# Low parts of the MLP weights: an adding transfer onto the negated rounded part instead of a VectorE difference

## The chip, the core and the metric

The kernel runs on one core of a Trainium2 chip. The metric is the device time of one execution in microseconds (us); the lower the better. TensorE (PE), VectorE (DVE), ScalarE (ACT), GpSimd (POOL) and SyncE (SP, which here only issues transfers) run side by side and wait for each other by semaphores; 16 DMA engines move the data.

## The reference

A model of three blocks over 512 tokens of width 1024 in float32. Two blocks hold a mixer (mLSTM and a convolution branch) and an MLP, each under a modulation that comes from a conditioning vector; a third block has a windowed attention and a gated convolution. What the change touches is the MLP of the two first blocks:

```python
for l in range(DEPTH):                      # DEPTH = 2
    mod = c_act @ w_ada[l] + b_ada[l]       # six vectors of 1024
    ...                                     # mixer
    h = rms_norm(x, g_pre_mlp[l]) * (1 + sc_mlp) + sh_mlp
    f = jnp.square(jax.nn.relu(h @ w_ff1[l])) @ w_ff2[l]   # 1024 -> 4096 -> 1024
    x = x + gt_mlp * rms_norm(f, g_post_mlp[l])
```

## The kernel before

**Split products.** Every large product of float32 numbers is made from three fast ones. A number is split into a rounded part h (type float32r) and a low part lo = x - h, and `mm3` (L163) accumulates h*h, h*lo and lo*h in PSUM. Activations are split where they are made, weights where they are loaded.

**A weight unit.** `wunit` (L145) makes one unit of 128 x 1024 numbers, 512 KB: SP loads it into `raw`, one of three buffers of the ring `wr`; ACT rounds it into `h` (ring `wh`, four buffers, L155); `sub` (L142) writes `lo = raw - h` (ring `wl`, four buffers, L143) on DVE, or on POOL where `eng=P` is given. The raw buffer is free when the difference is done. A unit then feeds 24 matmuls of 512 columns. After the unit `wunit` calls `step()`.

**Gemvs beside the products.** `step()` advances a list `pending` of generators, which compute the modulation of later stages. Most are gemvs (L348): each step loads 512 KB of `w_ada` or `w_mod_2` into the same ring `wr` (L352), and DVE scales it and adds it to an accumulator (L360, L362), once for `w_ada` and twice for the two vectors of `mod2_pairs`. A gate's gemv ends in a row that POOL broadcasts to all partitions (L413). In the first MLP `pending` holds gemvs of 8, 16, 16 and 8 steps. In the second it holds gemvs of 8 and 16 steps and then 24 steps of `expand_bias`, small copies between DRAM tensors that use no raw buffer.

**The MLP** (`mlp`, L534). `proj_first` uses four units that the mixer's end has loaded. `ff1(c)` computes eight tiles of the hidden layer with `projA` (L247): for each group of 256 columns two units, one for each half of the 1024 inputs, then 16 x 3 matmuls into two PSUM banks; `cons` applies Relu and Square on ACT and splits the result on DVE. `projB_chunk` (L289) multiplies finished hidden tiles with `w_ff2`: one unit feeds four PSUM banks, one for each 128 tokens. The order is ff1 chunks 0 and 1, a `projB_chunk` of 8 tiles, ff1 chunk 2, 8 tiles, ff1 chunk 3, 10 tiles. Then come `reload()` of x, `drain()` of what is pending and `projB_tail` (L310), whose six units lie in buffers outside the rings; during it the units of the next stage are loaded.

**Order.** SP issues in program order (a manual schedule). On the other engines the framework's scheduler sets the order, and the buffer that each tile gets from a ring, by its own estimates when the kernel is built; each engine then executes its queue in order.

Of the kernel before, what the change touches and what calls it, by code (L numbers as in the profile page):

```python
# [8 lines left out]
F32 = mybir.dt.float32  # L9
F32R = mybir.dt.float32r  # L10
BF16 = mybir.dt.bfloat16
I32 = mybir.dt.int32
AF = mybir.ActivationFunctionType
ALU = mybir.AluOpType
# [32 lines left out]
def fused_blocks_kernel(ctx: ExitStack, tc: tile.TileContext, I, out):  # L47
    nc = tc.nc
    V, S, P, PE, SP = nc.vector, nc.scalar, nc.gpsimd, nc.tensor, nc.sync
    act = S.activation  # L50
# [17 lines left out]
    def A(shape, dt=F32, name="a"):  # L68
        if not free_slots:
            raise RuntimeError(str(sorted(t.name for _, t in slot_of.values())))  # L70
        s = free_slots.pop(0)
        t = ap.tile(shape, dt, tag=f"A{s}", name=name)
        slot_of[id(t)] = (s, t)
        return t

    def HL(n, name):
        return A([128, 2, n], F32R, name)

    def free(*ts):
        for t in ts:  # L80
            free_slots.append(slot_of.pop(id(t))[0])
# [4 lines left out]
    def t2(shape, dt=F32, name="t2"):  # L86
        return t2p.tile(shape, dt, tag="t2", name=name)
# [4 lines left out]
    def mm():  # L92
        return mmp.tile([128, 512], F32, tag="mm", name="mm")
# [36 lines left out]
    def step():  # L130
        while pending:
            try:
                next(pending[0])
                return
            except StopIteration:
                pending.pop(0)

    def drain():
        while pending:
            step()  # L140

    def sub(dst, x_, h, eng=None):  # L142
        (eng or V).tensor_tensor(dst, x_, h.bitcast(F32), op=ALU.subtract)  # L143

    def wunit(src, a, b, eng=None, slots=False):  # L145

        raw = wrp.tile([128, a, b], F32, tag="wr", name="wr")
        SP.dma_start(raw, src)
        if slots:
            h = A([128, a, b], F32R, "wha")  # L150
            lo = A([128, a, b], F32R, "wla")
        else:
            h = whp.tile([128, a, b], F32R, tag="wh", name="wh")
            lo = wlp.tile([128, a, b], F32R, tag="wl", name="wl")
        S.copy(h, raw)  # L155
        sub(lo, raw, h, eng)
        step()
        return h, lo

    def unitsA(wv, c0, eng=None):  # L160
        return [wunit(wv[:, u * 4:u * 4 + 4, c0:c0 + 256], 4, 256, eng) for u in range(wv.shape[1] // 4)]

    def mm3(ps, ah, al, bh, bl, first, last):  # L163
        PE.matmul(ps, ah, bh, start=first, stop=False)  # L164
        PE.matmul(ps, ah, bl, start=False, stop=False)  # L165
        PE.matmul(ps, al, bh, start=False, stop=last)  # L166
# [69 lines left out]
    def mmA(ps, units, m, hT, view=lambda v: v, us=None):  # L236

        n = len(units)
        c = slice(m * 128, m * 128 + 128)
        for u in us or range(n):  # L240
            h, lo = units[u]
            for kk in range(4):
                kt = 4 * u + kk
                mm3(view(ps), h[:, kk, c], lo[:, kk, c], view(hT[kt][:, 0]), view(hT[kt][:, 1]),
                    kt == 0, kt == 4 * n - 1)

    def projA(wv, cols, hT, consumer, eng=None):  # L247

        ps = []
        for c0 in cols:  # L250
            un = unitsA(wv, c0, eng)
            pp = [mm(), mm()]
            for m in range(2):
                mmA(pp[m], un, m, hT)
            ps += pp
        consumer(ps)
# [17 lines left out]
    def proj_first(units, hT, between, consumer, perm=False):  # L274

        ps = [mm() for _ in range(2 * len(units))]
        for hf in range(2):
            def view(v, hf=hf):
                return grid(v)[:, :, 4 * hf:4 * hf + 4] if perm else v[:, hf * 256:hf * 256 + 256]

            for u in range(2):
                for ci, un in enumerate(units):
                    for m in range(2):
                        mmA(ps[2 * ci + m], un, m, hT, view, (u,))
            if hf == 0:
                between()
        consumer(ps)

    def projB_chunk(wv, kts, acts, evac, eng=None, hook=None):  # L289

        nk = len(kts)
        for n in range(2):
            ps = [mm() for _ in range(4)]
            for u in range(nk // 2):
                k0 = kts[2 * u]
                h, lo = wunit(wv[:, k0:k0 + 2, n * 512:n * 512 + 512], 2, 512, eng)
                for t in range(4):
                    for k in range(2):
                        kk = 2 * u + k
                        a = acts[kts[kk]]  # L300
                        mm3(ps[t], a[:, 0, t * 128:t * 128 + 128], a[:, 1, t * 128:t * 128 + 128],
                            h[:, k], lo[:, k], kk == 0, kk == nk - 1)
                if hook:
                    hook()
            if n == 1:
                free(*(acts[k] for k in kts))
            for t in range(4):
                evac(t, n, ps[t])

    def projB_tail(wv, kts, acts, y, G, eng=None, scale=1.0, prefetch=None, post=None):  # L310

        nk = len(kts)
        units = [[wunit(wv[:, kts[2 * u]:kts[2 * u] + 2, n * 512:n * 512 + 512], 2, 512, eng, True)
                  for u in range(nk // 2)] for n in range(2)]
        if prefetch:
            prefetch()
        for t in range(4):
            ps = [mm(), mm()]
            if t == 3 and post:
                post(-1)  # L320
            for n in range(2):
                for kk in range(nk):
                    h, lo = units[n][kk // 2]
                    a = acts[kts[kk]]
                    mm3(ps[n], a[:, 0, t * 128:t * 128 + 128], a[:, 1, t * 128:t * 128 + 128],
                        h[:, kk % 2], lo[:, kk % 2], kk == 0, kk == nk - 1)
            if t == 3:
                for un in units:
                    for h, lo in un:
                        free(h, lo)  # L330
                free(*(acts[kts[kk]] for kk in range(nk)))
            for n in range(2):
                c = slice(n * 512, n * 512 + 512)
                V.tensor_tensor(y[t][:, c], ps[n], y[t][:, c], op=ALU.add)
            yg = [t2([128, 512], F32, "yg") for _ in range(2)]
            for n in range(2):
                c = slice(n * 512, n * 512 + 512)
                V.tensor_tensor(yg[n], y[t][:, c], G[:, c], op=ALU.mult)
            r = row_rstd(y[t], scale)
            for n in range(2):  # L340
                c = slice(n * 512, n * 512 + 512)
                V.scalar_tensor_tensor(x[t][:, c], yg[n], r, x[t][:, c], op0=ALU.mult, op1=ALU.add)
            free(y[t])
            if post:
                post(t)
# [163 lines left out]
    def reload(src=lambda t: xd[t]):  # L509
        for t in range(4):  # L510
            x[t] = A([128, 1024], F32, f"x{t}")
            SP.dma_start(x[t], src(t))
# [21 lines left out]
    def mlp(l, pre, units, nxt, pre_next):  # L534
        w1 = I["w_ff1"][l].rearrange("(k p) n -> p k n", p=128)
        w2 = I["w_ff2"][l].rearrange("(k p) n -> p k n", p=128)
        hid = {}

        def cons(k0):
            def f(ps):  # L540
                for m in range(len(ps)):
                    s = t2([128, 512], F32, "s")
                    act(s, ps[m], AF.Relu)  # L543
                    act(s, s, AF.Square)  # L544
                    o = HL(512, "hid")
                    V.tensor_copy(o[:, 0], s)  # L546
                    sub(o[:, 1], s, o[:, 0])
                    hid[k0 + m] = o
            return f

        def ff1(c, lo=0):
            for g in range(lo, 4):
                projA(w1, [c * 1024 + g * 256], hT, cons(c * 8 + g * 2))

        proj_first(units, pre.hT, lambda: pre.turn(1), cons(0))
        hT = pre.hT
        ff1(0, len(units))
        ff1(1)
        projB_chunk(w2, range(8), hid, ev_first)
        ff1(2)  # L560
        projB_chunk(w2, range(8, 16), hid, ev_add)
        ff1(3)
        free(*hT)
        projB_chunk(w2, range(16, 26), hid, ev_add)
        reload()
        drain()
        G = mods[l, 5]
        projB_tail(w2, range(26, 32), hid, y, G, prefetch=pre_next, post=nxt.post)
        free(G)
# [862 lines left out]
```

## Time and profile before

| | |
|---|---|
| median of 3 runs | 2289.1 us (2287.65 to 2289.36) |
| the profiled execution | 2287.2 us, span of its instructions 2285.2 us |
| busy share of the span | PE 98%, DVE 67%, ACT 43%, POOL 13% |
| the 16 DMA engines | 277.69 MB moved; 37.8% of their time on the one hardware queue |
| first MLP, second MLP | about 436 to 750 us, about 1176 to 1500 us |

PE is the engine for matmuls, PEld its weight loads. A row of a group gives line, engine, operation, output and inputs by the program's names, shape and count, then busy us, mean ns of one, and behind the bar the engine's idle time just before these instructions with what ended most of it. A timeline row gives start and duration in us, and in brackets the engine's idle time before it and what ended it. Matmuls are pipelined and their ends are modelled, so the duration of one is longer than the distance of two. A few per cent of the matmul records can be missing.

### The profile page before, as it was taken

The page shows a single profiled execution, that of the slowest core. Times are in us where ns is not written, and L with a number is a line of the kernel's source. Part 1 is how long each engine was busy: PE and PEld are TensorE (multiplying, and loading weights), DVE is VectorE, ACT ScalarE, POOL GpSimd, SP SyncE. Part 2 cuts the span into 40 slices and gives each one's busy share as a digit, 9 for nine tenths or more (in the row PEclk, how much of TensorE's full clock was granted, in tenths as well). Part 3 has the DMA queues.
Part 4 walks back from the last instruction along what each step waited for, and adds up shares of the span by engine and source line. Part 5 has one row for each costly group of instructions (what it writes and reads, how often), then busy time and mean ns, then how long its engine had stood idle before and what let it go on. Part 6 is the DMA issues. An engine that isn't in the chain of part 4 may idle for free.

```text
span 2285.2 us, 29859 instructions
## 1 busy us (share of the span) xinstructions
PE 2240.0 (98%) x11164; PEld 1807.5 (79%) x11164; DVE 1530.7 (67%) x3037; ACT 979.1 (43%) x1651; POOL 301.3 (13%) x263
## 2 busy tenths in 40 slices
PE   8999999999999999999999999999999999999998
PEld 3777677878777888767887778888888888878886
DVE  4898998874555678899887643387566574652345
ACT  3557554543323334666543332235545554222232
POOL 1763000000000144400000000000321311000000
PEclk9999999999999999999999999999999999999999
DMA  7632134366565232321436544523211321532331
GB/s 265 211 116 79 55 120 131 128 198 194 179 190 176 87 117 85 92 65 47 148 120 187 177 127 127 170 75 114 88 50 54 98 77 60 172 95 94 99 131 65
DMA packets 194585, 277.69 MB, mean 122 GB/s; under 512 B 13812, under 2 KB 146548, under 8 KB 194440
## 3 DMA queue, kind: packets, MB, share of 16 engines
q1 hardware_dynamic: 194440, 275.78, 37.8%
q8 instruction: 88, 1.44, 0.3%
q14 instruction: 57, 0.47, 0.1%
HBM read 263.68 MB, written 14.37 MB: 122 GB/s over the span
## 4 chain that ended last, share of the span: by engine, by line
PE 74%; DVE 5%; ACT 2%; issue 1%; DMA 0%; POOL 0%; SPq 0%; DVEq 0%; ACTq 0%; POOLq 0%
PE mm L166 22%; PE mm L165 22%; PE mm L164 22%; PE cv L1129 1%; PE tr L1114 1%; PE mm L827 1%; PE mm L851 1%; PE mm L1093 0%; PE mm L1095 0%; DVE h L143 0%; PE tr L218 0%; DVE nt L176 0%; ACT sb L1103 0%; DVE h L231 0%; ACT junk L195 0%
## 5 line engine op out<-in xcount | busy, mean ns | idle before, releaser
L164 PE MATMUL mm<-h,wh 128*128 128x512 f32 (+1 forms) x1728 | 656.8, 381 | 3.8 <-DVE h L231 2.9
L165 PE MATMUL mm<-h,wh 128*128 128x512 f32 (+1 forms) x1728 | 654.3, 379 | 0.7 <-DVE h L143 0.6
L166 PE MATMUL mm<-h,wl 128*128 128x512 f32 (+1 forms) x1728 | 654.4, 379 | 0.1
L155 ACT CAST wh<-wr 128x1024 fp32r<-128x1024 f32 (+1 forms) x318 | 323.3, 1018 | 532.4 <-PE mm L165 249.7
L143 DVE TENSOR_TENSOR wl<-wr,wh 128x1024 fp32r<-128x1024 f32 x254 | 314.0, 1240 | 224.4 <-ACT wh L155 223.4
L164 PEld LDWEIGHTS mm<-h,wh 128*128 128x128 f32 x1728 | 324.7, 188 | 75.2 <-DVE h L231 6.8
L166 PEld LDWEIGHTS mm<-h,wl 128*128 128x128 f32 x1728 | 324.8, 188 | 68.3 <-issue 5.9
L165 PEld LDWEIGHTS mm<-h,wh 128*128 128x128 f32 x1728 | 325.3, 188 | 66.1 <-issue 3.0
L589 DVE SCALAR_TENSOR_TENSOR cv<-glu,vec,cv 128x511 f32<-128x511 f32 (+24 forms) x480 | 327.8, 732 | 7.1 <-ACT cv L584 6.8
L362 DVE SCALAR_TENSOR_TENSOR acc<-wr,csil,acc 128x1024 f32<-128x1024 f32 x91 | 116.1, 1284 | 127.6 <-DMA wr<-in_w_ada_dram 88.4
L165 PE MATMUL mm<-wl,hid 128*128 128x512 f32 x416 | 164.2, 395 | 0.0
L166 PE MATMUL mm<-wh,hid 128*128 128x512 f32 x416 | 164.1, 395 | 0.0
L164 PE MATMUL mm<-wh,hid 128*128 128x512 f32 x416 | 163.4, 395 | 0.0
L143 POOL TENSOR_TENSOR wl<-wr,wh 128x1024 fp32r<-128x1024 f32 (+1 forms) x68 | 137.8, 2033 | 185.0 <-ACT wh L155 144.4
L413 POOL PARTITION_BROADCAST G<-row x5 | 8.3, 1665 | 699.5 <-DVE row L410 383.4
L164 PEld LDWEIGHTS mm<-wh,hid 128*128 128x128 f32 x416 | 78.2, 188 | 19.9 <-issue 0.8
L166 PEld LDWEIGHTS mm<-wh,hid 128*128 128x128 f32 x416 | 78.2, 188 | 18.4
L165 PEld LDWEIGHTS mm<-wl,hid 128*128 128x128 f32 x416 | 78.2, 188 | 18.2
L543 ACT ACTIVATE s<-mm 128x512 f32<-128x512 f32 x64 | 38.0, 594 | 111.3 <-PE mm L166 111.3
L1103 ACT ACTIVATE sb<-sb,nm 128x512 f32<-128x512 f32 x64 | 46.4, 725 | 59.1 <-DVE nm L1101 50.2
L1083 POOL TENSOR_TENSOR bias<-band,amask 128x256 f32<-128x256 f32 x48 | 43.3, 910 | 206.5 <-DVE mx L1098 131.1
L546 DVE CAST hid<-s 128x512 fp32r<-128x512 f32 x64 | 29.0, 457 | 45.9 <-ACT s L544 45.9
(318 smaller groups left out, 3659.4 us busy)
## 6 DMA issues: line engine op xcount, KB each, us to landing
wr<-in_w_in_dram SPq DMA_DIRECT2D x140, 512.0 KB
wr<-in_w_ff_dram SPq DMA_DIRECT2D x128, 512.0 KB
wr<-in_w_ada_dram SPq DMA_DIRECT2D x80, 512.0 KB
wr<-in_w_out_dram SPq DMA_DIRECT2D x32, 512.0 KB
wr<-in_w_mod_dram SPq DMA_DIRECT2D x24, 512.0 KB
wr<-in_w_ada_dram SPq DMA_DIRECT2D x32, 256.0 KB
xd<-x SPq DMA_DIRECT2D x16, 512.0 KB
x<-xd SPq DMA_DIRECT2D x16, 512.0 KB
```

The costliest lines, as they stand in the source:

```text
L143: (eng or V).tensor_tensor(dst, x_, h.bitcast(F32), op=ALU.subtract)
L155: S.copy(h, raw)
L164: PE.matmul(ps, ah, bh, start=first, stop=False)
L165: PE.matmul(ps, ah, bl, start=False, stop=False)
L166: PE.matmul(ps, al, bh, start=False, stop=last)
L362: V.scalar_tensor_tensor(acc, raw, cv[:, kt:kt + 1], acc, op0=ALU.mult, op1=ALU.add)
L543: act(s, ps[m], AF.Relu)
L546: V.tensor_copy(o[:, 0], s)
L589: V.scalar_tensor_tensor(pa[m][:, s:], at[:, m, :512 - s], vv("wdw", l * 248 + (2 * g + m) * 31 + j, 1), pa[m][:, s:], op0=ALU.mult, op1=A ...
L827: PE.matmul(ps[:, :n], k[h][:, kt, j * 128:j * 128 + 128], q[h][:, kt, j * 128:], start=kt == 0, stop=kt == 1)
L1083: P.tensor_tensor(btile[:, b].rearrange("p (c r) -> p c r", r=8), bands[i][:, hh, :, o:o + 32].rearrange("p r c -> p c r"), amask[:, var, ...
L1103: act(sb, sb, AF.Exp, bias=nm, accum_out=sm)
```

## The change

Where `wunit` is called with `eng="dma"`, the difference on DVE is replaced by two steps. ACT writes the negated rounded part into `lo`. Then POOL issues a transfer that reads `raw` and adds it to `lo` in place, so that lo = -h + raw. The argument is given in `ff1` and in the three `projB_chunk` calls of both MLPs: 54 units in each. The units of `proj_first` and `projB_tail`, of the mixers and of the third block stay as they are.

```diff
--- before.py
+++ after.py
@@ -153,7 +153,11 @@
             h = whp.tile([128, a, b], F32R, tag="wh", name="wh")
             lo = wlp.tile([128, a, b], F32R, tag="wl", name="wl")
         S.copy(h, raw)
-        sub(lo, raw, h, eng)
+        if eng == "dma":
+            act(lo, h.bitcast(F32), AF.Copy, scale=-1.0)
+            P.dma_start(lo, raw.bitcast(F32R), accum_op=ALU.add)
+        else:
+            sub(lo, raw, h, eng)
         step()
         return h, lo
 
@@ -550,18 +554,18 @@
 
         def ff1(c, lo=0):
             for g in range(lo, 4):
-                projA(w1, [c * 1024 + g * 256], hT, cons(c * 8 + g * 2))
+                projA(w1, [c * 1024 + g * 256], hT, cons(c * 8 + g * 2), "dma")
 
         proj_first(units, pre.hT, lambda: pre.turn(1), cons(0))
         hT = pre.hT
         ff1(0, len(units))
         ff1(1)
-        projB_chunk(w2, range(8), hid, ev_first)
+        projB_chunk(w2, range(8), hid, ev_first, "dma")
         ff1(2)
-        projB_chunk(w2, range(8, 16), hid, ev_add)
+        projB_chunk(w2, range(8, 16), hid, ev_add, "dma")
         ff1(3)
         free(*hT)
-        projB_chunk(w2, range(16, 26), hid, ev_add)
+        projB_chunk(w2, range(16, 26), hid, ev_add, "dma")
         reload()
         drain()
         G = mods[l, 5]
```

## Rows read from the trace of the kernel before

**Rows 1.** Page, part 1: busy us (share of the span) xinstructions.

```profile
PE 2240.0 (98%) x11164; PEld 1807.5 (79%) x11164; DVE 1530.7 (67%) x3037; ACT 979.1 (43%) x1651; POOL 301.3 (13%) x263
```

**Rows 2.** Busy time by window; columns in the first line.

```profile
core 0: us, PE busy (x) PEld busy (x) DVE busy (x) ACT busy (x) POOL busy (x), PEclk, DMA share, GB/s
0.00:60.00 60.00, 48.99 (x181) 21.56 (x182) 28.37 (x93) 19.05 (x40) 10.36 (x11) 0.91 0.75 253
500.00:560.00 60.00, 60.00 (x260) 48.56 (x259) 32.99 (x35) 17.48 (x22) 1.30 (x1) 1.00 0.58 188
1360.00:1420.00 60.00, 60.00 (x260) 48.55 (x259) 21.81 (x25) 14.68 (x17) 0.00 (x0) 1.00 0.40 125
```

**Rows 3.** Groups by line, 440 to 740 us: busy, mean ns | idle before.

```profile
L164 PE MATMUL mm<-h,wh 128*128 128x512 f32 (+1 forms) x256 | 97.8, 383 | 0.7 <-DVE h L231 0.7
...
L143 DVE TENSOR_TENSOR wl<-wr,wh 128x1024 fp32r<-128x1024 f32 x54 | 65.3, 1222 | 19.6 <-ACT wh L155 19.2
L155 ACT CAST wh<-wr 128x1024 fp32r<-128x1024 f32 x54 | 56.8, 1052 | 133.1 <-PE mm L166 79.8 <-PE mm L165 42.2 <-DMA wr<-in_w_ff_dram 8.4
...
L546 DVE CAST hid<-s 128x512 fp32r<-128x512 f32 x32 | 14.4, 454 | 7.1 <-ACT s L544 7.1
```

**Rows 4.** Waits of SP's DMA queue: us in total, times, longest us.

```profile
SPq L148 <- DVE wl L143: 680.3, 161, 21.0
```

**Rows 5.** Timeline of ACT, 480 to 496 us: start us, us, instruction.

```profile
483.63 1.05 ACT L155 CAST wh<-wr 128x1024 fp32r<-128x1024 f32 x1 [1.30 <-PE mm L165]
486.42 1.05 ACT L155 CAST wh<-wr 128x1024 fp32r<-128x1024 f32 x1 [1.74 <-PE mm L165]
...
494.80 1.05 ACT L155 CAST wh<-wr 128x1024 fp32r<-128x1024 f32 x1 [1.30 <-PE mm L165]
```

**Rows 6.** Line 356: instructions, duration ns min/median/max.

```profile
L356 ACT ACTIVATE wr<-wr,csil x14: 1142/1153/1169, 64.2 to 131.5; 128x1024 f32<-128x1024 f32 x14
```

**Rows 7.** Timeline of POOL, 440 to 740 us.

```profile
505.68 1.30 POOL L413 PARTITION_BROADCAST G<-row  x1 [109.10 <-DVE row L410]
```

**Rows 8.** Timeline of SP, then DVE: one gemv load and its use.

```profile
494.68 0.33 SPq L352 DMA_DIRECT2D wr<-in_w_ada_dram  x1
...
498.24 1.29 DVE L362 SCALAR_TENSOR_TENSOR acc<-wr,csil,acc 128x1024 f32<-128x1024 f32 x1 [1.13 <-DMA wr<-in_w_ada_dram]
```

**Rows 9.** Timelines of DVE, SP, ACT, 448 to 466 us: the ring twice.

```profile
448.52 1.23 DVE L143 TENSOR_TENSOR wl<-wr,wh 128x1024 fp32r<-128x1024 f32 x1 [1.58 <-ACT wh L155]
...
458.06 1.22 DVE L143 TENSOR_TENSOR wl<-wr,wh 128x1024 fp32r<-128x1024 f32 x1
...
449.77 0.33 SPq L352 DMA_DIRECT2D wr<-in_w_ada_dram  x1
450.97 0.38 SPq L148 DMA_DIRECT2D wr<-in_w_ff_dram  x1
...
459.31 0.33 SPq L352 DMA_DIRECT2D wr<-in_w_ada_dram  x1
460.50 0.38 SPq L148 DMA_DIRECT2D wr<-in_w_ff_dram  x1
...
456.80 1.06 ACT L155 CAST wh<-wr 128x1024 fp32r<-128x1024 f32 x1 [0.93 <-DMA wr<-in_w_ff_dram]
...
464.90 1.05 ACT L155 CAST wh<-wr 128x1024 fp32r<-128x1024 f32 x1 [2.55 <-DMA wr<-in_w_ff_dram]
```

**Rows 10.** Timelines of DVE, SP, 534 to 537 us: buffers kept apart.

```profile
534.26 1.28 DVE L362 SCALAR_TENSOR_TENSOR acc<-wr,csil,acc 128x1024 f32<-128x1024 f32 x1 [2.74 <-DMA wr<-in_w_ada_dram]
535.46 1.22 DVE L143 TENSOR_TENSOR wl<-wr,wh 128x1024 fp32r<-128x1024 f32 x1
...
535.57 0.33 SPq L352 DMA_DIRECT2D wr<-in_w_ada_dram  x1
536.71 0.38 SPq L148 DMA_DIRECT2D wr<-in_w_ff_dram  x1
```

## The prediction

> **What bounds the kernel now.** The page comes first: PE is busy 2240.0 of 2285.2 us, and POOL 301 [rows 1]. An average says little about two stages, so the next view is the busy time by window. Inside the first MLP (500 to 560 us) PE is busy 60.00 of 60 us, and the same in the second MLP after its gemvs (1360 to 1420), where DVE works 21.8 us instead of 33.0 and PE starts the same 260 matrix multiplications [rows 2]. So here neither the amount of DVE work nor its place slows PE. The groups of 440 to 740 us say it again: before all the `h,wh` matmuls PE idled 0.7 us, for a `to_feat` product (L231), and no row has PE waiting for a low part; the 54 casts `wh` were late because PE had not yet released the buffer, 122.0 of their 133.1 us of idle time, and only 8.4 us for a load [rows 3]. DVE's 54 differences, 65.3 us, are all hidden.
>
> What is close to its limit is the ring `wr` of three raw buffers. SP's waits are led by "L148 <- DVE wl": 680.3 us, 161 times [rows 4]. The next load waits until a difference has released a raw buffer. That is harmless only while the buffer comes back in time, so the change is read there.
>
> **PE's demand.** A unit is 24 matmuls; `projA` takes two. Two casts that wait for the same release stand 11.17 us apart (483.63, 494.80), the second of a pair 2.79 us behind the first [rows 5]. PE thus takes a pair in 11.17 us. Four `wh`/`wl` buffers let a pair be made while the one before it is used: a low part is wanted 2.8 + 11.17 = 14.0 us after its cast starts.
>
> **What the change removes.** 54 DVE differences per MLP (28 units in `ff1`, 26 in the three `projB_chunk`), 108 in all, 1.22 us each. Worth at PE: the idle time that they cause, which is none. Even the 0.7 us is behind another product. Gain: 0, at most 1 us in each MLP.
>
> **What it adds on ACT.** One negated copy of 128x1024 behind each cast. The nearest row is the scaled Copy of the same size, 1.15 us [rows 6]. 54 x 1.15 = 62 us per 300 us stretch on an engine that is mostly waiting for PE there [rows 3]. Behind the copy, which also waits for a `wl` buffer, stand the next cast and the Relu that empties PSUM. Two of the four `mm` banks are spare for 11 us; priced at 0, and at 1.15 us per group if a bank were short.
>
> **What it adds on POOL.** An issue that waits for ACT. Behind it stand the next issues and `partition_broadcast`, which before sat alone on an idle POOL for 109 us until its row came [rows 7]. If the order puts a broadcast ahead of an issue too early, that issue waits for the gate's row: three times in both MLPs, a few us each, inside the 14 us lead. Priced at 0.
>
> **The adding transfer itself, T,** from the end of the negated copy to landing, has no row: before, POOL starts no transfers. It moves 512 KB, as a load does, and must read two operands. Lower end: the quickest plain 512 KB load here, issued 494.68 and used at 498.24, 3.6 us [rows 8]. Usual landing: 460.50 to the cast at 464.90, 4.4 us; late: 450.97 to 456.80, 5.8 [rows 9]. The second operand costs another pass at the fastest stretch's rate: 253 GB/s at share 0.75 is 337 GB/s when full [rows 2], so 524 KB take 1.6 us. I take T = 4.4 + 1.6 = 6.0. Upper end: two plain transfers one after the other, 2 x 4.4 = 8.8. I choose the middle because it has both the landing and the second read; SBUF instead of HBM as source may shorten it, issuing on POOL may lengthen it. The Trainium skill has a rule against this change: "SBUF — State Buffer", section on who interferes with whom, states that while DVE runs a 2-port operation, as an fp32 copy, GpSimd can't write the descriptors of its transfers. No run here shows it yet; by the 0.45 us of a cast L546 [rows 3] T would be 6.45 and the sum below 15 us higher.
>
> **The raw buffer's loop.** Before: cast 1.05 + difference 1.22, a raw buffer is held some 2.4 us past the start of its cast. After: cast 1.05 + copy 1.15 + T = 8.2 us, since the transfer reads the raw buffer till its end. While a gemv runs, every unit's load alternates with a gemv load in the ring, and SP keeps this order. Two patterns occur. Shared: the freed buffer takes the gemv load first, then the weight load; from the difference's end to the next cast but one it took 449.75 to 456.80 (7.05 us) and 459.28 to 464.90 (5.6), mean 6.3 [rows 9]. Own buffers: around 535 us each gemv load follows the gemv's own operation and each weight load its difference [rows 10]; then only the landing counts, mean of 4.4 and 5.8, 5.1. A loop brings two units. Before: 6.3 + 2.4 = 8.7 us, below 11.17. After: 6.3 + 8.2 = 14.5 or 5.1 + 8.2 = 13.3; mean 13.9, which is 2.7 us over PE's 11.17.
>
> **The sum.** Gemv loads run beside 48 of the first MLP's units (four generators: 8 + 16 + 16 + 8) and 24 of the second's (8 + 16). First MLP: 24 pairs x 2.7 = 65, less the spare lead 14.0 - 8.2 = 6, so 59 us. Second: 12 x 2.7 = 32 - 6 = 26 us. Without gemv loads three units share a loop of 5.1 + 8.2 = 13.3 us against 16.8: no loss, and lost PE time is not won back. Together +85 us. The profiled execution took 2287.2 us around a span of 2285.2; it stands 1.9 under the median 2289.1. 2287.2 + 85 + 1.9 = 2374.
>
> **Ends.** T = 3.6: hold 5.8, loops 12.1 and 10.9, mean 11.5; 24 x 0.33 = 8, all in the spare lead of 8.2: +0, 2289. T = 8.8: hold 11.0, loops 17.3 and 16.1, mean 16.7; 24 x 5.5 - 3 = 129, 12 x 5.5 - 3 = 63: +192, 2481. One microsecond of T is worth some 34 us.
>
> **Rivals.** (a) **The ring still closes**, not slower. In the mean of the two patterns a loop is 5.7 + 2.2 + T; it equals 11.17 us at T = 3.3, and the spare lead takes the loss below 4.6 us up to T = 3.8; with own buffers alone (5.1 + 2.2 + T) up to T = 4.4. So it decides at a T of about 4 us. For it speaks the lower row, and that no HBM is read; against it the second operand. It gives 2289. The Trainium skill, "DMA: Bandwidth & Descriptors", section "Anatomy of one DMA", gives a fit for POOL's transfers of 2.0 us + bytes/436 GB/s; for 512 KB that is an estimate of 3.2 us, and by it nothing is lost. The fit is for plain copies. (b) **The DMA engines fill up.** They are busy 0.58 with gemv loads [rows 2]. A transfer per 5.59 us adds 1.6 us in one pass (0.28) or 3.1 in two (0.56): 0.86 to 1.14. At 1.14 loads and sums queue behind each other, and landing and T go to the upper end: 2481, or beyond if adding is slower than moving. (c) **Faster**: only if freeing DVE shortened a wait of PE. There are 0.7 us to win per MLP; 2288. For it speaks nothing in these windows; other stages are not touched.
>
> **How the numbers follow.** The measurement tells about 0.2% (4.6 us) from no change. Forecast, the ring comes back late by 1 to 4 us per pair (2300 to 2430): 0.55. Rival (b), 2430 and up: 0.24. Rival (a): 0.17. Rival (c), or gains elsewhere over 4.6 us: 0.04. Slower is 0.55 + 0.24 = 0.79, same 0.17, faster 0.04. The range from 2287 to 2490 takes in both ends of T and leaves out the far part of (b) and part of (c).
>
> **What would show it.** In the profile of the changed kernel: PE's busy share in 500 to 560 us falls to some 0.8, and before `h,wl` or `wl,hid` matmuls stands an idle time that a DMA ended; SP's lead wait is on the adding transfer instead of "DVE wl"; a casts' pair comes every 13 to 14 us during the gemvs and every 11.2 after them; the second MLP loses about half of the first's. DVE's L143 `wl` falls by 108, ACT gains 108 copies of about 1.15 us, and POOL starts 108 transfers. I am wrong if the casts still wait for PE (T short), if the loss goes on after the gemvs (T above about 9, or engines full), if the copy is held up behind a Relu on ACT, or if the granted clock falls with the new gaps: it was 1.00, all at the level of 2.4 GHz, in the windows of both MLPs, and 0.91, so partly at 1.2 GHz, in the first 60 us, where PE was busy 49.0 us [rows 2].

## The result, and the profile after

The changed kernel takes 2413.9 us (median of 4 runs, 2405.5 to 2421.8), the kernel before 2289.2 us beside it: ratio 1.054, 95% interval 1.051 to 1.058, that is +125 us. Forecast was 2374 us in a range of 2287 to 2490, slower. The profiled execution of the changed kernel took 2415.3 us around a span of 2413.5.

The page of the changed kernel: busy us by engine (against [rows 1]), the queue of the new transfers (packets, MB, share of 16 engines), two groups, and the transfer with its median us to landing.

```profile
PE 2274.6 (94%) x11164; PEld 1824.2 (76%) x11164; DVE 1408.5 (58%) x2929; ACT 1086.3 (45%) x1759; POOL 395.6 (16%) x371
...
q0 software_dynamic: 15552, 56.63, 12.8%
...
L158 POOL DMA_DIRECT2D wl<-wr x108 | 94.6, 876 | 785.1 <-ACT wl L157 749.2
...
L157 ACT ACTIVATE wl<-wh 128x1024 fp32r<-128x1024 f32 x108 | 114.4, 1059 | 2.7
...
wl<-wr POOLq DMA_DIRECT2D x108, 512.0 KB, 6.3
```

DVE has 108 instructions less, ACT 108 copies of 1.06 us and POOL 108 issues of 0.88 us more. PE starts the same 11164 matmuls and is idle 138.9 us instead of 45.2 (span less busy). One adding transfer holds the engines 2.86 us (12.8% of 2413.5 us, over 108).

Busy time by window, after; columns in the first line. The last two rows are the two MLPs, each from one spill of x (SP's writes of x to DRAM, `xd<-x`) to the next.

```profile
core 0: us, PE busy (x) PEld busy (x) DVE busy (x) ACT busy (x) POOL busy (x), PEclk, DMA share, GB/s
500.00:560.00 60.00, 50.80 (x197) 38.97 (x196) 21.46 (x27) 27.68 (x34) 9.60 (x10) 0.91 0.85 228
1480.00:1540.00 60.00, 60.00 (x260) 48.58 (x259) 10.14 (x16) 24.45 (x28) 8.66 (x10) 1.00 0.92 218
412.00:847.00 435.00, 379.72 (x1663) 302.65 (x1662) 153.00 (x284) 179.97 (x239) 59.89 (x60) 0.94 0.79 210
1221.00:1640.00 419.00, 380.31 (x1685) 304.04 (x1684) 147.44 (x278) 182.16 (x241) 48.83 (x55) 0.95 0.78 198
```

The same two stages in the kernel before:

```profile
411.00:773.00 362.00, 359.37 (x1664) 291.43 (x1663) 214.00 (x339) 128.02 (x186) 12.17 (x6) 1.00 0.54 175
1148.00:1512.00 364.00, 363.25 (x1684) 295.79 (x1683) 208.99 (x332) 128.15 (x186) 2.26 (x1) 1.00 0.48 150
```

The whole difference lies in the two MLPs: 362 to 435 us and 364 to 419 (by the start of the spills, to 0.1 us: +73.3 and +54.7, together 128.0 of the 128.3 by which the spans differ). Where [rows 2] had PE busy 60.00 of 60 us at 500, it is now 50.80; at 1480, with no gemv beside, PE is full again. Of the 128 us, 52.7 + 37.9 are PE's idle time (435 - 379.72 less 362 - 359.37, and so on), and 20.4 + 17.1 are longer busy time for the same matmuls: the granted clock fell from 1.00 to 0.94 and 0.95, so part of them ran at 1.2 instead of 2.4 GHz.

Timelines of ACT, POOL and SP of the changed kernel (start us, us, instruction, in brackets idle time before it and what ended it): the start of the first MLP's gemv stretch, one turn of the ring, a cast near that stretch's end, then the start and the end of the second's.

```profile
445.64 1.05 ACT L155 CAST wh<-wr 128x1024 fp32r<-128x1024 f32 x1 [0.99 <-PE mm L169]
...
472.46 1.05 ACT L155 CAST wh<-wr 128x1024 fp32r<-128x1024 f32 x1 [7.47 <-DMA wr<-in_w_ff_dram]
473.54 1.06 ACT L157 ACTIVATE wl<-wh 128x1024 fp32r<-128x1024 f32 x1
...
486.11 1.05 ACT L155 CAST wh<-wr 128x1024 fp32r<-128x1024 f32 x1 [7.17 <-DMA wr<-in_w_ff_dram]
...
756.12 1.05 ACT L155 CAST wh<-wr 128x1024 fp32r<-128x1024 f32 x1 [1.29 <-PE mm L169]
...
1258.12 1.05 ACT L155 CAST wh<-wr 128x1024 fp32r<-128x1024 f32 x1 [1.01 <-PE mm L169]
...
1452.93 1.05 ACT L155 CAST wh<-wr 128x1024 fp32r<-128x1024 f32 x1 [1.28 <-PE mm L169]
...
1464.07 1.05 ACT L155 CAST wh<-wr 128x1024 fp32r<-128x1024 f32 x1 [1.28 <-PE mm L169]
...
474.90 0.85 POOL L158 DMA_DIRECT2D wl<-wr  x1 [9.91 <-ACT wl L157]
...
482.18 0.38 SPq L148 DMA_DIRECT2D wr<-in_w_ff_dram  x1
```

This is the loop of the prediction, row by row. The cast starts at 472.46, the copy ends at 474.60, POOL issues at 474.90; at 482.18 the raw buffer is back and SP issues the next load, 9.7 us after the cast's start (2.4 before); 3.9 us later the next cast but one starts, 13.65 us after the first. In [rows 5] that distance was 11.17 us and the releaser was PE; now it is the load. From 445.64 to 756.12 the first MLP makes 22 pairs in 310.5 us, 14.1 each; from 1258.12 to 1452.93 the second makes 14 in 194.8 us, 13.9 each. Behind the gemvs the pitch, the distance of two pairs, is 11.14 us again and PE the releaser.

Waits of SP's DMA queue and of PE, after: the first row in 440 to 740 us, the others of the whole run (us in total, times, longest).

```profile
SPq L148 <- DMA wl<-wr: 132.5, 35, 7.2
...
PE tr L382 <- ACT rows L379: 25.9, 4, 11.0
PE mm L170 <- DMA wl<-wr: 17.8, 11, 3.0
PE mm L168 <- DVE y L535: 16.3, 4, 6.3
PE mm L168 <- ACT y L526: 13.1, 3, 5.1
PE mm L168 <- ACT s L547: 9.8, 2, 5.0
PE mm L169 <- DMA wl<-wr: 7.8, 3, 5.2
```

SP's longest wait in the stretch is now for the adding transfer. PE waits directly for a low part only 25.6 us (17.8 + 7.8). 65.1 us stand in rows that the kernel before doesn't have: `rows`, a small copy of a gemv's result on ACT, and `y` and `s`, the copies, additions and Relus that empty PSUM. They come late where they stand in the order of ACT or DVE behind an operation whose load had not landed. A Relu started at 545.52, right behind the cast of 544.57 that waited for its load, and PE stood idle from 541.38 to 546.17; in the same way the `y` of 686.59 stood on DVE behind a gemv operation (685.39), and PE was idle from 681.12 to 687.42. So much of the lateness of the loads reaches PE by way of these two queues. Whether the copy `rows` is a cause of its own is asked below.

### The profile page after: what moved, and what is told of

The parts are those of the page before. It is cut to its first block, busy times and chain, and to the rows that moved or that the text cites. A ratio compares the mean times of both kernels' runs of the same rounds, so it can differ in the third digit from the quotient of the medians.

```text
span 2413.5 us, 30211 instructions
## 1 busy us (share of the span) xinstructions
PE 2274.6 (94%) x11164; PEld 1824.2 (76%) x11164; DVE 1408.5 (58%) x2929; ACT 1086.3 (45%) x1759; POOL 395.6 (16%) x371
## 3 DMA queue, kind: packets, MB, share of 16 engines
q0 software_dynamic: 15552, 56.63, 12.8%
## 4 chain that ended last, share of the span: by engine, by line
PE 60%; DMA 21%; DVE 8%; issue 7%; ACT 4%; SPq 0%; POOL 0%; POOLq 0%; DVEq 0%; ACTq 0%
PE mm L170 17%; PE mm L169 17%; PE mm L168 17%; DMA wl<-wr 8%; DMA wr<-in_w_ff_dram 8%; DMA wr<-in_w_ada_dram 3%; PE mm L831 1%; PE mm L855 1%; PE cv L1133 1%; PE tr L1118 1%; DVE acc L366 1%; DVE h L143 1%; PE cv L443 1%; ACT wh L155 1%; DVE h L235 0%
## 5 line engine op out<-in xcount | busy, mean ns | idle before, releaser
L170 PE MATMUL mm<-h,wl 128*128 128x512 f32 (+1 forms) x1728 | 660.2, 383 | 17.9 <-DMA wl<-wr 17.8
L143 DVE TENSOR_TENSOR wl<-wr,wh 128x1024 fp32r<-128x1024 f32 x146 | 182.9, 1254 | 147.0 <-ACT wh L155 146.4
L158 POOL DMA_DIRECT2D wl<-wr x108 | 94.6, 876 | 785.1 <-ACT wl L157 749.2
L168 PE MATMUL mm<-wh,hid 128*128 128x512 f32 x416 | 167.8, 409 | 25.7 <-ACT s L547 9.8
L169 PE MATMUL mm<-wl,hid 128*128 128x512 f32 x416 | 169.6, 408 | 7.8 <-DMA wl<-wr 7.8
L170 PE MATMUL mm<-wh,hid 128*128 128x512 f32 x416 | 168.9, 406 | 0.0
L168 PEld LDWEIGHTS mm<-wh,hid 128*128 128x128 f32 x416 | 81.2, 195 | 48.7 <-ACT s L547 11.1
L157 ACT ACTIVATE wl<-wh 128x1024 fp32r<-128x1024 f32 x108 | 114.4, 1059 | 2.7
L170 PEld LDWEIGHTS mm<-wh,hid 128*128 128x128 f32 x416 | 81.4, 196 | 19.5
```

The source lines that it names most:

```text
L157: act(lo, h.bitcast(F32), AF.Copy, scale=-1.0)
L158: P.dma_start(lo, raw.bitcast(F32R), accum_op=ALU.add)
```

## The experiments

Theory A, that of the prediction: the raw buffer is held until the adding transfer has landed, and in the ring of three that it shares with the gemv loads the loop becomes longer than PE's pair. B: the transfer's traffic lengthens all loads and sums, whatever is held. C: the added work on ACT delays casts and Relus.

**The copy on ACT alone** (C). The difference becomes the negated copy on ACT and an addition on DVE; no transfer.

```diff
-            P.dma_start(lo, raw.bitcast(F32R), accum_op=ALU.add)
+            V.tensor_tensor(lo, raw, lo.bitcast(F32), op=ALU.add)
```

> The ACT copy alone: ACT writes the negated rounded part, and DVE adds the raw part to it; no transfer. Held 1.05 + 1.06 + 1.22 + some 0.2 = 3.5 us, loop 6.3 + 3.5 = 9.8 us at most. Theory A: nothing lost, 2286 to 2293 us. Theory C (the copies on ACT hold up the Relus and the copies out of PSUM by themselves): 2310 us and more.

Measured: 2289.2 us, ratio 1.0003 (0.9993 to 1.0012). C is out as a cause by itself: where the loads come in time, 108 copies cost nothing. Its window:

```profile
500.00:560.00 60.00, 60.00 (x260) 48.49 (x259) 34.78 (x36) 28.58 (x35) 2.25 (x1) 1.00 0.62 192
```

ACT is busier than in the changed kernel (28.58 us against 27.68), and PE is full.

**The buffer given back early, with the same traffic.** The copy reads the raw buffer and the transfer reads the rounded part.

```diff
-            act(lo, h.bitcast(F32), AF.Copy, scale=-1.0)
-            P.dma_start(lo, raw.bitcast(F32R), accum_op=ALU.add)
+            act(lo, raw, AF.Copy, scale=-1.0)
+            P.dma_start(lo, h, accum_op=ALU.add)
```

> The changed kernel with the hold of the raw buffer taken away and the transfers kept: ACT writes the negated raw part into the low part, so the raw buffer is free after the cast and this copy (2.1 us), and the adding transfer reads the rounded part instead. Same size, same number, same queue, same wait. The low part comes out with the other sign; all else is computed as before. Theory A (the raw buffer's loop is the cause): a loop of about 6 + 2.1 = 8 us against 11.2 us of PE, so nearly all of the 125 us goes: 2287 to 2305 us. Theory B (the engines' capacity: 108 adding transfers fill the 16 DMA engines): traffic is the same, so the time stays at 2390 to 2420 us. Theory C (the ACT copy, or POOL's issues): stays too.

Measured: 2376.2 us, ratio 1.039 (1.037 to 1.041), +88. Neither theory alone gave this. 38 us come back, and in 500 to 560 us PE is busy 55.0 us instead of 50.8, but past 560 it falls to 46.6 of 60. The timelines of SP and DVE there show another loop:

```profile
564.84 0.33 SPq L356 DMA_DIRECT2D wr<-in_w_ada_dram  x1
565.26 0.39 SPq L148 DMA_DIRECT2D wr<-in_w_ff_dram  x1
570.92 0.33 SPq L356 DMA_DIRECT2D wr<-in_w_ada_dram  x1
...
569.61 1.28 DVE L366 SCALAR_TENSOR_TENSOR acc<-wr,csil,acc 128x1024 f32<-128x1024 f32 x1 [4.80 <-DMA wr<-in_w_ada_dram]
577.32 1.29 DVE L366 SCALAR_TENSOR_TENSOR acc<-wr,csil,acc 128x1024 f32<-128x1024 f32 x1 [6.43 <-DMA wr<-in_w_ada_dram]
```

A gemv load issued at 564.84 is used at 569.61, and only when DVE is done with it, at 570.89, does SP issue the next one; in SP's order the next weight load stands behind it. So one gemv step, and the one unit that goes with it, takes 6.1 us here (564.84 to 570.92) and the next 7.7 (570.92 to 578.61, the end of its use), while PE needs 5.6 for a unit. The gemv load took 3.6 us in [rows 8] and takes 4.8 and 6.4 here. So B has a part: with the transfers the loads land later, and with one buffer circling among the gemv loads that is enough.

**The hold without the traffic.** POOL writes the difference, once and then once more to the same place, after a copy on ACT; no transfer.

```diff
-            act(lo, h.bitcast(F32), AF.Copy, scale=-1.0)
-            P.dma_start(lo, raw.bitcast(F32R), accum_op=ALU.add)
+            act(lo, raw, AF.Copy)
+            sub(lo, raw, h, P)
+            sub(lo, raw, h, P)
```

> A smaller hold without transfers, and DVE left free: in the 108 units ACT copies the raw part into the low part (1.06 us), then POOL makes the difference twice (2.4 to 2.8 us each). Held: 1.05 + 1.06 + about 5.2 = 7.3 us; POOL is busy 10.4 of 11.2 us per pair of units at most. Theory A (hold and landing make a loop that must fit into PE's 11.2 us): own buffers 4.4 to 5.1 + 7.3 = 12, shared 6.3 + 7.3 = 13.6; 2310 to 2365 us. Theory B (the engines' capacity alone): nothing is added to them, 2287 to 2295 us.

Measured: 2415.0 us, ratio 1.056 (1.054 to 1.059): by the number the changed kernel's time, with none of its transfers. By stage too: the second MLP loses 55.0 us, there 54.7. That it is the same number is luck, as the last two rows show. Window, then the timelines of ACT and POOL:

```profile
500.00:560.00 60.00, 43.55 (x177) 33.31 (x176) 36.23 (x27) 21.52 (x28) 39.95 (x17) 0.89 0.44 135
```

```profile
490.07 1.05 ACT L155 CAST wh<-wr 128x1024 fp32r<-128x1024 f32 x1 [4.68 <-DMA wr<-in_w_ff_dram]
...
497.28 1.05 ACT L155 CAST wh<-wr 128x1024 fp32r<-128x1024 f32 x1 [3.05 <-DMA wr<-in_w_ff_dram]
...
510.88 1.05 ACT L155 CAST wh<-wr 128x1024 fp32r<-128x1024 f32 x1 [2.23 <-DMA wr<-in_w_ff_dram]
...
492.64 4.90 POOL L143 TENSOR_TENSOR wl<-wr,wh 128x1024 fp32r<-128x1024 f32 x2 [1.62 <-ACT wl L157]
...
531.90 1.78 POOL L418 PARTITION_BROADCAST G<-row  x1 [6.00 <-issue]
...
540.70 15.60 POOL L143 TENSOR_TENSOR wl<-wr,wh 128x1024 fp32r<-128x1024 f32 x6 [7.01 <-issue]
```

The DMA engines are busy only 0.44, less than before the change, and PE still loses. The hold is 7.5 us (490.07 to 497.54) and two units take 13.6 us from 497.28 (13.9 on the mean of 483 to 525). From release to cast that leaves 13.9 - 7.5 = 6.4 us, the shared pattern of [rows 9]. But POOL, which makes the low parts here, also stands idle 6.0 us ahead of a gate row's broadcast and 7.0 us behind it, and the low parts behind it come late. At the three broadcasts of the two MLPs PE waits 13.5, 9.3 and 12.2 us for a low part, 35 us that the changed kernel doesn't have. So the hold by itself costs some 91 us here (126 - 35, an estimate), more than the 76 at the end of the expected range: it is most of the loss, and this run doesn't show that it is all of it.

The run also tells what the traffic does to the gemv loads. From issue to use in the first MLP, where DVE waited for them, they took 4.1 us on the mean in the kernel before and 4.1 here without transfers, 5.2 in the changed kernel and 5.5 in the run with the early release.

**A longer hold** (the same with a third difference, on DVE).

```diff
+            sub(lo, raw, h)
```

> The opposite: the hold kept and the transfers taken away. In the same 108 units ACT writes a copy of the raw part into the low part (1.06 us), then POOL makes the difference twice (2.4 us each) and DVE once more (1.2 us), one after the other since all write the same buffer; the raw buffer is held 1.05 + 1.06 + 2.4 + 2.4 + 1.2 = 8.1 us, as in the changed kernel (8.4), with no transfer added. Theory A: loop about 6 + 8.1 = 14 us per two units against 11.2: 2345 to 2410 us. Theory B: nothing is added to the DMA engines: 2287 to 2300 us.

Measured: 2526.8 us, ratio 1.104 (1.102 to 1.106). It can't be used as a point on A's line, since the hold came out longer than meant. Timeline of DVE:

```profile
488.36 3.35 DVE L143 TENSOR_TENSOR wl<-wr,wh 128x1024 fp32r<-128x1024 f32 x1
492.84 1.22 DVE L143 TENSOR_TENSOR wl<-wr,wh 128x1024 fp32r<-128x1024 f32 x1
```

The difference that usually takes 1.22 us took 3.35 while POOL ran differences, and the raw buffer was held 11 to 14 us. Only the direction fits.

**Buffers given back to the loop.** Gemv loads get a ring of their own with two buffers; the weights have all three of `wr`. One slot and two temporary buffers make the room; the control takes these away alone.

```diff
-NSLOT = 35
+NSLOT = 34
+    wgp = ctx.enter_context(tc.tile_pool(name="wgp", bufs=2))
-    t2p = ctx.enter_context(tc.tile_pool(name="t2p", bufs=8))
+    t2p = ctx.enter_context(tc.tile_pool(name="t2p", bufs=6))
-            raw = ... else wrp.tile([128, 1024], F32, tag="wr", name="wr")
+            raw = ... else wgp.tile([128, 1024], F32, tag="wg", name="wr")
```

> The changed kernel with the loads of the gemvs in a ring of their own (two buffers), so that the weights have all three raw buffers; to make room, one slot and two small temporary buffers fewer (the next kernel has these alone). Theory A: three units share a loop of 6 + 8.4 = 14.4 us against 16.8 us of PE: most of the loss goes, 2290 to 2325 us. Theory B: the traffic is the same: 2390 to 2420 us.

> The changed kernel with one slot and two small temporary buffers fewer, the ring unchanged. Both theories: as the changed kernel, 2400 to 2430 us; the difference to the split rings is what the split is worth.

Measured: split 2330.5 us, ratio 1.019 (1.017 to 1.021); control 2436.8 us, ratio 1.065 (1.063 to 1.067). Both lie 5 to 7 us above their ranges; the control is 23 us slower than the changed kernel, so the room that was taken away has a price of its own. Against the control the split is worth 106 us. The same window in both, split first:

```profile
500.00:560.00 60.00, 60.00 (x259) 47.51 (x258) 24.36 (x29) 31.00 (x38) 11.38 (x13) 1.00 1.04 290
```

```profile
500.00:560.00 60.00, 45.67 (x185) 34.38 (x183) 22.01 (x28) 24.55 (x33) 9.00 (x9) 0.92 0.82 210
```

With the full traffic of gemv loads, weights and sums the DMA share is 1.04 at 290 GB/s, and PE is full. So in this window the engines' capacity, rival (b), doesn't set the changed kernel's time; the ring does.

**A fourth shared buffer**, without a ring for the gemvs.

```diff
-NSLOT = 35
+NSLOT = 34
-    wrp = ctx.enter_context(tc.tile_pool(name="wrp", bufs=3))
+    wrp = ctx.enter_context(tc.tile_pool(name="wrp", bufs=4))
```

> The changed kernel with four raw buffers in the shared ring instead of three (one slot fewer). Weight and gemv loads alternate, so each kind gets two; the weights had two already. Theory A: the weights' loop of two units stays 4 to 5 us of landing and 9.7 us held, against 11.2: 2390 to 2425 us. If a buffer more helps whoever gets it (all four shared): loop 13.9 x 3/4 = 10.4 us, 2290 to 2330 us.

Measured: 2368.9 us, ratio 1.036 (1.033 to 1.039), between the two ranges. In 500 to 560 us PE is busy 57.1 of 60 us, but from 555 us on the long pairs are back. Timeline of ACT:

```profile
555.25 1.05 ACT L155 CAST wh<-wr 128x1024 fp32r<-128x1024 f32 x1 [6.97 <-DMA wr<-in_w_ff_dram]
...
568.92 1.05 ACT L155 CAST wh<-wr 128x1024 fp32r<-128x1024 f32 x1 [6.09 <-DMA wr<-in_w_ff_dram]
```

A pair of 13.7 us with four buffers, and the next is 13.9: which of them carry weights and which gemvs changes along the way. A fourth buffer in the shared ring helps less (-45) than a ring of one's own (-83). But the split has five raw buffers in all; five in a shared ring were not run, so how much of the difference is the separation is not shown.

**Split rings and early release together.**

```diff
+            act(lo, raw, AF.Copy, scale=-1.0)
+            P.dma_start(lo, h, accum_op=ALU.add)
...
+            raw = ... else wgp.tile([128, 1024], F32, tag="wg", name="wr")
```

> The split rings and the early release together: three raw buffers for the weights, two for the gemvs, the raw buffer free after the ACT copy, the adding transfer reads the rounded part (the low part comes out with the other sign). The traffic of the changed kernel is all there. Theory A: both parts of the loop are gone, 2287 to 2310 us. Theory B (the engines' capacity is what is left of the loss): as the split rings alone, 2325 to 2335 us.

Measured: 2335.6 us, ratio 1.020 (1.018 to 1.021), the same as the split alone. Once the weights have three buffers, the hold costs nothing more. Both stay some 42 to 46 us behind the kernel before, so that rest is not the hold. It is the time that theory B forecast here (2325 to 2335), so a share of the traffic in this rest is not excluded.

**What the second operand costs.** A plain transfer in place of the adding one; the subtraction is left out.

```diff
-            P.dma_start(lo, raw.bitcast(F32R), accum_op=ALU.add)
+            P.dma_start(lo, raw.bitcast(F32R))
```

> The changed kernel with a plain transfer instead of the adding one: POOL moves the raw part over the low part, which leaves out the subtraction. It tells what the second operand costs. The adding transfer kept the engines busy 2.86 us each (12.8% of 2413.5 us by 108), a plain load 1.62 us per 512 KB. Theory A: T from 6.3 to about 5, the loads land sooner too; some 30 to 55 us less than the changed kernel, 2355 to 2385 us. If adding is what makes the transfer slow beyond its second read, the transfer lands in under 4 us and the time falls to 2300 us.

Measured: 2345.5 us, ratio 1.025 (1.023 to 1.027), 68 us below the changed kernel and below theory A's range. Its page:

```profile
q0 software_dynamic: 15552, 56.63, 6.9%
...
L158 POOL DMA_DIRECT2D wl<-wr x108 | 58.0, 537 | 752.1 <-ACT wl L157 684.1
...
wl<-wr POOLq DMA_DIRECT2D x108, 512.0 KB, 4.3
```

Engine time of one is 1.49 us (6.9% of 2339.7 us, over 108) instead of 2.86, the issue 0.54 instead of 0.88, the landing 4.3 instead of 6.3. So T is 2.0 us shorter in the landing and 0.3 in the issue, and 68 us for 2.0 to 2.3 us are 30 to 34 us per microsecond of T, where the prediction had worked out some 34. The engines carry less traffic here too, so the run doesn't separate T from the landing of the loads. By the fit of the Trainium skill, "DMA: Bandwidth & Descriptors", section "Anatomy of one DMA", this transfer would take 3.2 us, an estimate. Measured beside the loads is 4.3, and 6.3 with the addition; the measurement decides.

**Only the units without gemv loads beside.** The transfer in 36 units (the last 6 of the first MLP's 54, the last 30 of the second's), the difference on DVE in the others.

```diff
+            i = (nunit[0] - 1) % 54
+            beside = i < (48 if nunit[0] <= 54 else 24)
+            use, eng = not beside, None
```

> The change only in the 36 units beside which no gemv load runs (the last 6 of the first MLP, the last 30 of the second); the other 72 keep the difference on DVE. The prediction priced these at nothing: three units share a loop of 5 + 8.4 us against 16.8 us. Theory A: 2287 to 2300 us. If the small copies between DRAM tensors (expand_bias) or the transfers by themselves cost PE time here, 2300 to 2325 us.

Measured: 2307.4 us, ratio 1.008 (1.007 to 1.010), +18 where the prediction had nothing: 6.1 in the first MLP, 15.9 in the second (the rest a little shorter). Timelines of ACT, POOL and PE at the main place (line numbers are 2 to 8 higher here):

```profile
1443.92 0.60 ACT L555 ACTIVATE s<-mm 128x512 f32<-128x512 f32 x1 [6.10 <-PE mm L178]
...
1445.08 1.04 ACT L157 CAST wh<-wr 128x1024 fp32r<-128x1024 f32 x1
1448.11 0.60 ACT L555 ACTIVATE s<-mm 128x512 f32<-128x512 f32 x1 [1.98 <-PE mm L178]
1448.60 1.05 ACT L165 ACTIVATE wl<-wh 128x1024 fp32r<-128x1024 f32 x1
...
1449.95 0.90 POOL L166 DMA_DIRECT2D wl<-wr  x1 [14.51 <-ACT wl L165]
...
1454.47 0.80 PE L177 MATMUL mm<-wl,hid 128*128 128x512 f32 x1 [5.21 <-DMA wl<-wr]
```

The cast waits for no load: it stands in ACT's order behind the Relu of a product, and its copy behind the next Relu. So the low part, complete 9.4 us after the cast's start, has no lead of 14 us; PE waits 5.2 us for it. Small copies between DRAM tensors run beside it (`expand_bias`). A further 8.6 us, in four waits up to 4.3, PE waits for `y` on DVE; in the longest it stands behind differences of the units that follow, whose casts waited for their loads.

**The same without the last 14 units of the second MLP** (22 units in all).

```diff
+            use, eng = not beside and not (nunit[0] > 54 and i >= 40), None
```

> As e6_no_gemv, less the 14 last units of the second MLP, beside and behind which the eight copies of zfull run: the adding transfer is left in 22 units (6 in the first MLP, 16 in the second beside the small zc copies). If the 18 us that e6_no_gemv lost belong to the stretch of zfull (its copies lengthen landings, and the casts stand behind Relus in ACT's queue there), nothing is left: 2286 to 2293 us. If every unit with the transfer costs PE time: about 18 x 22/36 = 11 us, 2300 us.

Measured: 2293.7 us, ratio 1.0016 (1.0007 to 1.0025), +4.5 by the medians. So some 14 of the 18 us belong to those 14 units. Whether ACT's order, the small copies or the loads of the units that follow bring the most of it, no run here separates.

**The copy that PE waits for.** The small copy `rows` moved from ACT to DVE in the changed kernel.

```diff
-        S.copy(rows, ps)
+        V.tensor_copy(rows, ps)
```

> The changed kernel with the copy of a gemv's column sums out of PSUM (rows, in colsum) on DVE instead of ACT. In the changed kernel PE waited 25.9 us, 4 times, for this copy, which stood in ACT's queue behind a cast whose load had not landed. Theory D (the queue's order on ACT adds to the loss): 2385 to 2405 us. Theory A alone (PE is short of weights anyway, a wait that goes comes back as another): 2405 to 2420 us.

Measured: 2411.1 us, ratio 1.053 (1.052 to 1.055), no change beside the changed kernel's 2413.9. Its longest wait of PE:

```profile
PE tr L382 <- DVE rows L379: 24.6, 3, 11.4
```

The same wait now carries DVE's name. Timeline of ACT at its longest in the changed kernel:

```profile
633.49 1.05 ACT L155 CAST wh<-wr 128x1024 fp32r<-128x1024 f32 x1 [7.29 <-DMA wr<-in_w_ff_dram]
...
634.93 0.58 ACT L379 COPY rows<-tr 128x512 f32<-128x512 f32 x1
```

The gemv was ready, for PE had started its column sums at 622.12; the copy came only at 634.93, behind a cast that waited for its load. On DVE, in this run, it started at 632.37, behind a gemv operation (631.06) that waited for its load. So the copy only went from one queue that waits for the ring to another. What it would be worth in a queue that waits for no load, this run doesn't show.

## Why the prediction was right, and where its terms were off

- **PE is full, and the differences on DVE are worth nothing.** Right: with the copy on ACT and an addition on DVE the time is the same (2289.2), and in the changed kernel PE gains nothing where the loop fits (60.00 of 60 at 1480).
- **ACT's copy at 0.** Right, by the same run (1.06 us each, priced at 1.15). What stands behind it was priced at 0 as well, with two spare `mm` banks; that held only while the loads came in time. In the changed kernel PE waits 39 us for banks that `y` and `s` empty late (16.3 + 13.1 + 9.8). **POOL** at 0: the issue itself takes 0.88 us and starts 0.3 us after the copy; no run isolates the waits in its order.
- **T and the hold.** T was put at 6.0 us from the copy's end. In the loop shown it is 7.6 (474.60 to 482.18), and the median landing from the issue is 6.3. The hold is 9.7 instead of 8.2 us. The second read was taken as another pass, and the engine time did nearly double (1.49 to 2.86 us); the landings beside the full traffic are what came out longer.
- **The release to the next cast** was put at 5.1 or 6.3 us and is 3.9 in that turn. So the loop came out at 13.65 us (mean pitch 13.9 to 14.1) where 13.9 was forecast: two errors of the opposite sign, and the sum is right partly by luck. In the mean stand pairs that the ring alone didn't set: after PE's wait of 11.0 us for `rows` the cast of 644.72 waits for PE, 20.65 us behind that of 624.07.
- **The sum over pairs.** First MLP: 22 pairs took 310.5 us, which is 64.7 more than 22 x 11.17 (59 forecast). Second: 14 pairs took 194.8 us, 38.4 more than 14 x 11.17 (26 forecast). Both stretches begin and end with a cast that waits for PE, so the spare lead is the same at both ends and there is nothing to take off for it, where the prediction took 6 us off in each. Together 103 instead of 85.
- **"Without gemv loads: no loss"** is the step that failed. The run with those units alone lost 6.1 + 15.9 = 22 us in the MLPs. The prediction had named the mechanism as what would make it wrong (a copy held up behind a Relu) and had priced it at 0. 103 + 22 = 125 of the 128 us; that the two parts simply add is an assumption, and 3 us stay open (the first MLP's last two pairs beside gemvs, from 756 us on, are in neither part).
- **The granted clock** fell with the gaps, as named but not priced. PE's busy time in the two MLPs grew by 37.4 us. That is a share of the account, not 37.4 us beside the loop: during the gemvs the pairs follow the ring, and a slower matmul there fills what would be idle time. How much it adds at the ends of the gaps no run tells.
- **Rivals.** (a), the ring closes, that is the loop still fits into PE's pair, needed a T of about 4; it is 7.6 in the loop shown. Even the plain transfer's T, some 2.3 us less, is above it, and that kernel lost 56 us. (b), engines full: no, at share 1.04 PE is full. But the traffic counts in the other way that (b) names, longer landings: it makes the gemvs' own loop the limit when the hold is taken away. (c): no.
- **The rule on POOL's descriptors** ("SBUF — State Buffer", who interferes with whom, in the Trainium skill) was to add 15 us. The issue took 876 ns on the mean and 852 at the least, so nothing of 0.45 us shows in the issue; a delay behind it no run isolates.
- **Signs forecast.** PE's share in 500 to 560 us 0.85 (0.8), SP's lead wait in the MLP on the adding transfer, pairs of 13.7 during the gemvs and 11.1 after them: all seen. Not seen: that the second MLP loses half of the first's (54.7 to 73.3), and that PE's idle time stands mostly before low parts (25.6 us of some 90).
- **Left open:** the 42 to 46 us that the split rings still lose. By the spills of x, 14.4 and 20.2 us of it lie in the two MLPs and 8.9 outside them, where no unit has the transfer. Up to 22 of them fit the units without gemvs; the rest lies in longer landings or in the slot and the temporary buffers that the rings took (23 us in the control, with the shared ring), and no run separates these.

No version here beats the kernel before: with PE full in these windows nothing that only frees DVE can. The best form with the transfer is the split ring, 2330.5 us.

## What to carry to other kernels

When work moves from an engine to a transfer, price first how long the source buffer is held, to the landing and not to the issue, and put that into the loop of its ring beside the pitch of the engine that bounds; an engine at 67% that hides its work has nothing to give. Where two streams of loads share a ring in a fixed order, a longer hold in one stalls both, and a ring for each, with two buffers more in all, was worth 106 us here against its control; a fourth shared buffer gave back 45 and an earlier release 38. An engine that works its queue in order passes a late load on to all that stands behind it. So look for what the largest wait's operation stands behind before moving it: the row that named a copy on ACT named it on DVE after the move, with 24.6 us instead of 25.9.

## What the runs showed of the hardware that was not expected

- Adding costs a transfer nearly twice the engine time: 2.86 us against 1.49 for 512 KB within SBUF, 6.3 against 4.3 us to landing, and POOL's issue 0.88 against 0.54 us.
- A two-input operation of DVE on 128x1024 took 3.35 us beside POOL's differences and 1.22 alone (the run with the longer hold).
- Between a difference on POOL and a `partition_broadcast`, POOL stood idle 6.0 us, and 7.0 us from the broadcast to the next difference (the hold without the traffic).
- The DMA share reached 1.04 of the 16 engines over 60 us with PE busy all the time: a high share alone was no sign of a bound here.
